# Norm weights as one row spread by products with ones, an early table load, and one PSUM bank for each 32-row merge, in a hybrid DeltaNet / RWKV-7 / Mamba-2 layer

## The chip, the cores and the metric

The program runs on one core of a Trainium2 chip. The metric is the device time of one execution in microseconds. The kernel before takes 1450.17 us (median of three runs, 1448.45 to 1453.15).

Engines: TensorE (PE) multiplies, with its weight loads shown as PEld; VectorE is DVE, ScalarE is ACT, GpSimd is POOL, and SyncE is SP, which here only issues transfers. Each takes its instructions in order. PE writes to PSUM, eight banks of 128 partitions by 512 float32; the other data lie in SBUF.

## The reference

One layer: `h + rms_norm(mixed @ w_out)`, where `h` is 16 meta tokens and 1024 frames of 1024 channels (1040 rows), `hn = rms_norm(h, norm_pre)`, one projection `hn @ w_in` feeds three groups of heads, and `mixed` is what they give, 2048 wide.

```
rms_norm(x, w) = x * rsqrt(mean(x*x) + 1e-6) * w
DeltaNet (6 heads of 128), in chunks:
  A   = strict_lower((k*beta) k^T * decay)
  sol = (A + I)^-1 [v*beta, k*beta*exp(gc)]
  then a scan over the chunks with a 128x128 state
RWKV-7  (8 heads of 64):  S <- S diag(w) + (S a) b^T + v k^T
Mamba-2 (12 heads of 64): chunked scan
```

The two places that matter here are the norm at the start, with its weight `norm_pre` (1024 numbers), and the inverse `(A + I)^-1` of each DeltaNet chunk.

## The kernel before

`setup` loads the rows in nine tiles `x` (c = 0 the 16 meta tokens, c = 1 to 8 each 128 frames), and the weight `npre` as 128 equal rows, which is one transfer that reads the same 4 KB 128 times. `pack` holds small constants in 578 columns, the identity (`ident`) in the first 128. For each tile, ACT squares and sums (L249, the table of activation functions loads ahead of the first), DVE makes the inverse root in a chain of eleven small instructions for each group of tiles `XG` (L252 and the helper), multiplies the tile by it and by `npre` (L256), PE transposes it in two halves of four 128x128 blocks (L261, tile `xT`), ACT copies each half rounded to `hh` (L264), and DVE writes what was lost in the rounding to `hl` (L265). `xT` has two banks, so that the transposes of a tile wait until `hl` of the tile before is written. `b_low` then projects the first 128 columns (`pj`, 72 matmuls), and `scalars` the small ones (`pjs`).

After that a planner written in Python (`schedule`) interleaves units: six DeltaNet heads a0 to a5, four RWKV pairs b0 to b3, two Mamba halves c0 and c1, and at the end the output projection `po`. A unit first projects its columns (each product as three of rounded operands, `hh` and `hl` against two parts of a weight), then it runs its scan on one of two lanes, and projections of later units fill PE between its steps. The planner settles which unit's piece comes next. Each instruction's place on its engine is then settled by a scheduler at compile time, by priorities and its own estimate of what is ready when.

PSUM: four banks `proj` for projections, and two banks for each of the two lanes (`gen0`, `gen1`), handed out in turn by `self.ps`.

The inverse in a DeltaNet head works on two chunks of 64 side by side in 128 rows. A substitution on DVE inverts the 32x32 blocks. Two merges join them to 64: tile `am1` holds 16 products of 32x32 (eight column blocks for each half of the rows), ACT copies them, and `am2` holds 16 products, and eight more for the transposed part. Then `am4` and `am5` join the 64 to 128. Each half has its own bank before, `pair[0]` and `pair[1]`. All matmuls here are issued by one helper, so that the profile gives them line 97; the profile counts two PE instructions for one float32 product. RWKV pairs have the same two merges, `bm1` and `bm2`, with both halves in one bank.

Of the kernel before, what the change touches and what calls it, by code (L numbers as in the profile page):

```python
# [14 lines left out]
F32 = mybir.dt.float32  # L15
F32R = mybir.dt.float32r
I32 = mybir.dt.int32
AF = mybir.ActivationFunctionType
ALU = mybir.AluOpType
MUL, ADD, SUB, MAX = ALU.mult, ALU.add, ALU.subtract, ALU.max  # L20

D = 1024
# [49 lines left out]
def t0(c):  # L72
    return 0 if c == 0 else NM + 128 * (c - 1)


def nt(c):
    return NM if c == 0 else 128
# [24 lines left out]
class Trunk:  # L102
# [102 lines left out]
    def setup(self):  # L205
        nc, a, cp = self.nc, self.a, self.cp
        v, act = nc.vector, nc.scalar
        self.hh = self.hp.tile([128, KT, L], F32R, tag="hh", name="hh")
        self.hl = self.hp.tile([128, KT, L], F32R, tag="hl", name="hl")
        xt = []  # L210

        def load(c):
            t = self.one([128, D], f"x{c}")
            nc.sync.dma_start(t[: nt(c)], a["meta"] if c == 0 else a["x"][128 * (c - 1): 128 * c])
            xt.append(t)

        for c in range(4):
            load(c)
        npre = self.one([128, D], "npre")
        nc.sync.dma_start(npre, a["npre"].broadcast_to((128, D)))  # L220
        pk = cp.tile([128, sum(n for _, n in PACK)], F32, tag="pack", name="pack")
        nc.sync.dma_start(pk, a["pack"])
        o = 0
        for key, n in PACK:
            setattr(self, key, pk[:, o: o + n])
            o += n
        for key, n in (("ctap_a", 18), ("ctap_c", 14)):
            setattr(self, key, getattr(self, key).rearrange("p (i t) -> p i t", i=n))
        for c in range(4, 9):
            load(c)  # L230
        wraw = self.one([128, KT, 32], "ws_raw")
        nc.sync.dma_start(wraw, a["ws"])
        self.ws = w = self.one([128, KT, 64], "ws_hl", F32R)
        nc.gpsimd.tensor_copy(w[:, :, 0:32], wraw)
        nc.gpsimd.tensor_tensor(w[:, :, 32:64], wraw, w[:, :, 0:32].bitcast(F32), SUB)
        self.pk2 = self.one([128, sum(n for _, n in PACK2)], "pack2")
        nc.sync.dma_start(self.pk2, a["pack2"])
        for key, n in (("dtb", 24), ("alog", 18), ("mbd", 12)):
            t = cp.tile([128, n], F32, tag="c_" + key, name="c_" + key)
            nc.sync.dma_start(t, a[key].broadcast_to((128, n)))  # L240
            setattr(self, key, t)
        ss = cp.tile([128, 9], F32, tag="xss", name="xss")
        rs = cp.tile([128, 9], F32, tag="xrs", name="xrs")
        v.memset(ss, 1.0)
        for cc in XG:
            for c in cc:
                n = nt(c)
                junk = self.one([128, D], "xjunk")
                act.activation(junk[:n], xt[c][:n], AF.Square, accum_out=ss[:n, c: c + 1])  # L249
            sl = slice(cc[0], cc[-1] + 1)  # L250
            with self.tc.high_priority(XP):
                v.tensor_scalar(ss[:, sl], ss[:, sl], 1.0 / D, EPS, MUL, ADD)  # L252
                self.rsqrt(rs[:, sl], ss[:, sl], "xr")
            for c in cc:
                n = nt(c)
                v.scalar_tensor_tensor(xt[c][:n], xt[c][:n], rs[:n, c: c + 1], npre[:n], MUL, MUL)  # L256
                for g in range(2):
                    p = self.ps(f"xT{c}_{g}")
                    for k in range(4):
                        kt = 4 * g + k  # L260
                        nc.tensor.transpose(p[:, k * 128: k * 128 + n], xt[c][:n, kt * 128: (kt + 1) * 128], self.ident[:n, :n])  # L261
                    pv = p.rearrange("p (k t) -> p k t", k=4)[:, :, :n]
                    sl = (slice(None), slice(4 * g, 4 * g + 4), slice(t0(c), t0(c) + n))
                    act.copy(self.hh[sl], pv)  # L264
                    v.tensor_tensor(self.hl[sl], pv, self.hh[sl].bitcast(F32), SUB)  # L265

        o = sum(n for _, n in PACK[:-HALVED])
        nc.gpsimd.tensor_scalar(pk[:, o:], pk[:, o:], 0.5, None, MUL)
        self.mu1 = cp.tile([128, 17], F32, tag="mu1", name="mu1")
        nc.gpsimd.tensor_scalar(self.mu1, self.mu, -1.0, 1.0, MUL, ADD)  # L270
        self.ka1 = cp.tile([128, 4], F32, tag="ka1", name="ka1")
        nc.gpsimd.tensor_scalar(self.ka1, self.ka, -1.0, 1.0, MUL, ADD)
# [96 lines left out]
    def unit_a(self, h):  # L369
        nc, sm = self.nc, self.sm  # L370
        v, act, pe, pool, sync = self.engines
# [17 lines left out]
        lo3 = lo[:, NM:].rearrange("p (c t) -> p c t", c=8)  # L389
# [11 lines left out]
        rs = sm.tile([128, 17], F32, tag="a_rs", name="a_rs", bufs=3)  # L401
        v.memset(ss[:, 0:1], 1.0)
        kdec = self.one([128, 8, 128], f"akd{h}")
        for cc, p in transposed(k, "akT", groups):
            for j, c in enumerate(cc):
                n = nt(c)
# [18 lines left out]
        for gi, cc in enumerate(groups):  # L425
            pk = self.ps(f"agk{h}_{gi}")
            for j, c in enumerate(cc):
                n, s = nt(c), t0(c)
                pe.matmul(pk[:n, j * 128: j * 128 + n], k[:, s: s + n], k[:, s: s + n], start=True, stop=True)
            for j, c in enumerate(cc):  # L430
                n, s = nt(c), t0(c)
# [32 lines left out]
        for cc, p in transposed(v_, "avT", groups):  # L464
            for j, c in enumerate(cc):
                n = nt(c)
# [11 lines left out]
        for gi, cc in enumerate(groups[:2]):  # L478
            gq = self.ps(f"agq{h}_{gi}")
            for j, c in enumerate(cc):  # L480
                s = t0(c)
# [7 lines left out]
        dd, v2 = dv[:, 0], dv[:, 1]  # L489
# [6 lines left out]
        v1 = dvf[:, 512:768], dvf[:, 0:256]  # L496
        fs = [(slice(64 * i, 64 * i + 32), slice(64 * i + 32, 64 * i + 64)) for i in range(2)]

        pair = [self.ps(f"am1{h}_{i}") for i in range(2)]
        for c in range(8):  # L500
            for i, (f, s) in enumerate(fs):
                pe.matmul(pair[i][s, 32 * c: 32 * c + 32], lo3[f, c, s], dd[f, c, 0:32], start=True, stop=True)
        for i, (f, s) in enumerate(fs):
            act.copy(v1[i][s], pair[i][s, 0:256])
        yield 0.6
        pair = [self.ps(f"am2{h}_{i}") for i in range(2)]
        for c in range(8):
            for i, (f, s) in enumerate(fs):
                pe.matmul(pair[i][f, 32 * c: 32 * c + 32], v1[i][s, 32 * c: 32 * c + 32], lo3[s, c, s], start=True, stop=True)
        f, s = fs[0]  # L510
        for c in range(8):
            pe.matmul(pair[0][s, 32 * c: 32 * c + 32], lo3[s, c, s], v1[0][s, 32 * c: 32 * c + 32], start=True, stop=True)
        act.copy(dd[s, :, 0:32], pair[0][s, 0:256].rearrange("p (c t) -> p c t", c=8))
        for i, (f, s) in enumerate(fs):
            act.copy(lo3[f, :, s], pair[i][f, 0:256].rearrange("p (c t) -> p c t", c=8))
        yield

        f, s = slice(0, 64), slice(64, 128)
        p = self.ps(f"am4{h}")
# [4 lines left out]
        p = self.ps(f"am5{h}")  # L524
# [16 lines left out]
        for c in range(9):  # L541
            n, s = nt(c), t0(c)
            if c:
                pk = self.ps(f"aks{h}_{c}")
# [44 lines left out]
        for gi in range(2):  # L589
            p = self.ps(f"aoT{h}_{gi}")  # L590
# [808 lines left out]
```

## Time and profile before

| | |
|---|---|
| median of three runs | 1450.17 us |
| the profiled execution | 1442.35 us, its span 1440.4 us |
| PE busy | 1389.7 us, 96% of the span |
| DVE busy | 935.4 us, 65% |
| ACT busy | 719.9 us, 50% |
| granted TensorE clock, mean | 0.985 of full speed |

The profile is one execution: the span goes from the first instruction to the last, and 1.95 us lie around it. Busy time is the time in which an engine has at least one instruction under way; overlapping matmuls count once. A line of the timeline merges equal instructions that follow each other (xN). In a window the clock is the mean of what was granted there. The windows show 1.00 up to 45 us, but transposes take twice as long in the first 25 us as later, so that there the figure is not the clock that the engine had.

### The profile page before, as it was taken

Reading aid. Unit: us, or ns where it says so; the run is one execution under the profiler, and the core shown is the slowest. Engines: PE = TensorE matmul, PEld = TensorE weight load, DVE = VectorE, ACT = ScalarE, POOL = GpSimd, SP = SyncE. Lnnn points to the kernel's source line nnn. Section 1 sums busy time; section 2 is a strip of 40 time slices with the busy share of each in tenths; the row PEclk is TensorE's granted clock in tenths of the full one; section 3 lists DMA queues with packets and bytes.
Section 4 is the critical chain, followed back from the end, with each engine's and each line's share of the span. In section 5 each row is a group of like instructions: output and inputs, shape, how many; then the busy total and the mean of one; then the engine's idle time right before and its main releaser. Section 6 shows DMA issues by size and latency. Waiting matters only on the chain.

```text
span 1440.4 us, 28351 instructions
## 1 busy us (share of the span) xinstructions
PE 1389.7 (96%) x10801; PEld 1188.8 (83%) x10801; DVE 935.4 (65%) x2610; ACT 719.9 (50%) x2020; POOL 172.4 (12%) x223
## 2 busy tenths in 40 slices
PE   4999999999999999999999999999999999899997
PEld 4999888778788789979778898889998987677786
DVE  6548586467667348879625788655589876632663
ACT  6365445446364464545636655444666355632520
POOL 2111010000010011111001110001231110201000
PEclk9999999999999999999979999999999999999999
DMA  7354243213234143234422242234553322743861
GB/s 233 78 131 87 56 102 71 57 40 88 44 66 112 30 133 89 57 82 89 100 60 60 54 108 62 59 88 89 133 124 77 71 38 56 233 133 101 254 198 44
DMA packets 120458, 136.43 MB, mean 95 GB/s; under 512 B 39867, under 2 KB 72379, under 8 KB 120323
## 3 DMA queue, kind: packets, MB, share of 16 engines
q1 hardware_dynamic: 102755, 102.64, 24.1%
q0 software_dynamic: 17568, 31.99, 13.4%
q8 instruction: 85, 1.39, 0.4%
q14 instruction: 50, 0.41, 0.1%
HBM read 116.99 MB, written 17.60 MB: 93 GB/s over the span
## 4 chain that ended last, share of the span: by engine, by line
PE 78%; issue 6%; ACT 6%; DMA 4%; DVE 4%; POOL 0%; SPq 0%; DVEq 0%; ACTq 0%; POOLq 0%
PE pj L97 45%; PE po L97 5%; PE bsi L97 4%; PE bu L97 3%; PE bgr L97 3%; PE am L97 2%; PE aops L97 1%; PE cdg L97 1%; ACT bbt L97 1%; DMA or<-in_w_out_dram 1%; PE ads L97 1%; PE av L97 1%; DMA omrw<-d_mix 1%; PE aks L97 1%; PE agk L97 1%
## 5 line engine op out<-in xcount | busy, mean ns | idle before, releaser
L97 PE MATMUL pj<-hh,w 128*128 128x350 f32 (+7 forms) x2736 | 757.6, 348 | 0.2 <-ACT hh L264 0.2
L97 PEld LDWEIGHTS pj<-hh,w 128*128 128x128 f32 x2736 | 483.4, 190 | 25.7 <-issue 4.4
L97 PE MATMUL pj<-hl,w 128*128 128x350 f32 (+7 forms) x1368 | 474.8, 347 | 0.0
L97 PEld LDWEIGHTS pj<-hl,w 128*128 128x128 f32 x1368 | 260.2, 190 | 11.8 <-issue 1.2
L153 POOL DMA_DIRECT2D w<-in_wt_dram x122 | 106.5, 873 | 878.6 <-ACT w L151 600.5
L151 ACT ACTIVATE w<-wr 128x512 fp32r<-128x512 f32 x122 | 76.8, 630 | 72.7 <-PE pj L97 70.7
L97 PE MATMUL po<-ow,omw 128*128 128x512 f32 x408 | 97.7, 400 | 4.0 <-ACT omw L1088 3.2
L97 PEld LDWEIGHTS po<-ow,omw 128*128 128x128 f32 x408 | 77.5, 191 | 24.2 <-ACT omw L1088 3.6
L97 PE MATMUL po<-ow,ome 128*128 128x512 f32 x360 | 90.5, 402 | 2.1 <-ACT ome L1088 1.6
L97 PEld LDWEIGHTS po<-ow,ome 128*128 128x128 f32 x360 | 66.6, 189 | 17.7 <-ACT ome L1088 2.2
L152 ACT CAST w<-wr 128x512 fp32r<-128x512 f32 x122 | 74.4, 609 | 0.1
L97 DVE TENSOR_SCALAR buv<-bu,b_ib 128x64 f32<-128x64 f32 x68 | 19.2, 282 | 71.6 <-PE bu L97 71.5
L97 PE MATMUL bsi<-buv,bgm 64*64 64x64 f32 x784 | 63.0, 230 | 0.7 <-DVE b_s L97 0.2
L97 DVE TENSOR_TENSOR s_tmp<-alb 33x30 f32<-33x30 f32 (+9 forms) x180 | 57.0, 317 | 3.2 <-DMA alb<-d_l 1.9
L97 DVE TENSOR_TENSOR alb<-alb,s_tmp 33x30 f32<-33x30 f32 (+9 forms) x180 | 57.0, 317 | 3.0 <-POOL alb L97 1.6
L97 PEld LDWEIGHTS bsi<-buv,bgm 64*64 64x64 f32 x784 | 43.5, 136 | 16.5 <-issue 4.6
L184 DVE SCALAR_TENSOR_TENSOR cbc<-pj,pack,cbc 128x346 f32<-128x346 f32 (+4 forms) x72 | 41.1, 571 | 20.5 <-ACT cbc L181 19.7
L852 ACT COPY by<-bsi 64x64 f32<-64x64 f32 x128 | 26.5, 207 | 48.9 <-PE bsi L97 47.6
L1089 DVE TENSOR_TENSOR ome<-omre,ome 128x512 fp32r<-128x512 f32 (+2 forms) x40 | 22.5, 600 | 36.2 <-ACT ome L1088 36.1
L97 PE MATMUL bgr<-bar,bbk 64*64 64x128 f32 x544 | 45.4, 277 | 0.0
L97 PE MATMUL bu<-buv,bbt 64*64 64x64 f32 x512 | 42.4, 234 | 0.0
L184 DVE SCALAR_TENSOR_TENSOR cx<-pj,pack,cx 128x346 f32<-128x346 f32 (+2 forms) x54 | 31.1, 576 | 16.9 <-ACT cx L181 15.9
(324 smaller groups left out, 2390.3 us busy)
## 6 DMA issues: line engine op xcount, KB each, us to landing
wr<-in_wt_dram SPq DMA_DIRECT2D x122, 256.0 KB, 3.4
w<-in_wt_dram POOLq DMA_DIRECT2D x122, 256.0 KB, 4.8
or<-in_w_out_dram SPq DMA_DIRECT2D x32, 256.0 KB, 3.8
omrw<-d_mix SPq DMA_DIRECT2D x32, 256.0 KB, 3.9
clt<-d_cs SPq DMA_DIRECT2D x24, 256.0 KB, 4.9
omre<-d_mix SPq DMA_DIRECT2D x24, 256.0 KB, 2.8
btw<-d_tw SPq DMA_DIRECT2D x8, 544.0 KB, 5.9
x<-in_x_dram SPq DMA_DIRECT2D x8, 512.0 KB, 7.7
```

The costliest lines, as they stand in the source:

```text
L97: return op(out, *args, **kw)
L151: nc.scalar.activation(w[:, 1], raw, AF.Copy, scale=-1.0)
L152: nc.scalar.copy(w[:, 0], raw)
L153: nc.gpsimd.dma_start(w[:, 1], src, accum_op=ADD)
L184: nc.vector.scalar_tensor_tensor(acc[:, a + z: b], p[:, o + z - s: o + b - a - s], cw[:, 3 - s: 4 - s], acc[:, a + z: b], MUL, ADD)
L852: nc.scalar.copy(yt[hs[(c - 1) % 2], (c - 1) // 2, hs[h]], pq[hs[h], 64:128])
L1089: nc.vector.tensor_tensor(t[:, 1], raw, t[:, 0].bitcast(F32), SUB)
```

## The change

The weight comes as one row of 1024 numbers by ACT's queue. Beside it in the same tile stand 128 ones, written by POOL and squared by ACT. Two products with one row in the contraction, ones against the row, put `npre` on 128 partitions of two `proj` banks, and L256 becomes two instructions of 512 columns that read the weight from PSUM. The square of the ones is the first activation in the program, so the table loads ahead of it. The identity comes by ACT's queue, the rest of `pack` by SP's. In the merges, both halves of `am1` share a bank, and both halves of `am2`.

```diff
--- before.py
+++ after.py
@@ -214,19 +214,28 @@
             nc.sync.dma_start(t[: nt(c)], a["meta"] if c == 0 else a["x"][128 * (c - 1): 128 * c])
             xt.append(t)
 
+
+        row = self.one([1, D + 128], "npre")
+        nc.scalar.dma_start(row[:, 0:D], a["npre"])
+        nc.gpsimd.memset(row[:, D:], 1.0)
+        act.activation(row[:, D:], row[:, D:], AF.Square)
         for c in range(4):
             load(c)
-        npre = self.one([128, D], "npre")
-        nc.sync.dma_start(npre, a["npre"].broadcast_to((128, D)))
         pk = cp.tile([128, sum(n for _, n in PACK)], F32, tag="pack", name="pack")
-        nc.sync.dma_start(pk, a["pack"])
+        nc.scalar.dma_start(pk[:, 0:128], a["pack"][:, 0:128])
+
+        npre = [self.pp.tile([128, 512], F32, tag="proj", name=f"npre{g}") for g in range(2)]
+        for g in range(2):
+            nc.tensor.matmul(npre[g], row[:, D:], row[:, 512 * g: 512 * g + 512], start=True, stop=True)
         o = 0
         for key, n in PACK:
             setattr(self, key, pk[:, o: o + n])
             o += n
         for key, n in (("ctap_a", 18), ("ctap_c", 14)):
             setattr(self, key, getattr(self, key).rearrange("p (i t) -> p i t", i=n))
-        for c in range(4, 9):
+        load(4)
+        nc.sync.dma_start(pk[:, 128:], a["pack"][:, 128:])
+        for c in range(5, 9):
             load(c)
         wraw = self.one([128, KT, 32], "ws_raw")
         nc.sync.dma_start(wraw, a["ws"])
@@ -253,8 +262,9 @@
                 self.rsqrt(rs[:, sl], ss[:, sl], "xr")
             for c in cc:
                 n = nt(c)
-                v.scalar_tensor_tensor(xt[c][:n], xt[c][:n], rs[:n, c: c + 1], npre[:n], MUL, MUL)
                 for g in range(2):
+                    xg = xt[c][:n, 512 * g: 512 * g + 512]
+                    v.scalar_tensor_tensor(xg, xg, rs[:n, c: c + 1], npre[g][:n], MUL, MUL)
                     p = self.ps(f"xT{c}_{g}")
                     for k in range(4):
                         kt = 4 * g + k
@@ -496,23 +506,23 @@
         v1 = dvf[:, 512:768], dvf[:, 0:256]
         fs = [(slice(64 * i, 64 * i + 32), slice(64 * i + 32, 64 * i + 64)) for i in range(2)]
 
-        pair = [self.ps(f"am1{h}_{i}") for i in range(2)]
+        p = self.ps(f"am1{h}")
+        for c in range(8):
+            for f, s in fs:
+                pe.matmul(p[s, 32 * c: 32 * c + 32], lo3[f, c, s], dd[f, c, 0:32], start=True, stop=True)
+        for i, (f, s) in enumerate(fs):
+            act.copy(v1[i][s], p[s, 0:256])
+        yield 0.6
+        p = self.ps(f"am2{h}")
         for c in range(8):
             for i, (f, s) in enumerate(fs):
-                pe.matmul(pair[i][s, 32 * c: 32 * c + 32], lo3[f, c, s], dd[f, c, 0:32], start=True, stop=True)
-        for i, (f, s) in enumerate(fs):
-            act.copy(v1[i][s], pair[i][s, 0:256])
-        yield 0.6
-        pair = [self.ps(f"am2{h}_{i}") for i in range(2)]
-        for c in range(8):
-            for i, (f, s) in enumerate(fs):
-                pe.matmul(pair[i][f, 32 * c: 32 * c + 32], v1[i][s, 32 * c: 32 * c + 32], lo3[s, c, s], start=True, stop=True)
+                pe.matmul(p[f, 32 * c: 32 * c + 32], v1[i][s, 32 * c: 32 * c + 32], lo3[s, c, s], start=True, stop=True)
         f, s = fs[0]
         for c in range(8):
-            pe.matmul(pair[0][s, 32 * c: 32 * c + 32], lo3[s, c, s], v1[0][s, 32 * c: 32 * c + 32], start=True, stop=True)
-        act.copy(dd[s, :, 0:32], pair[0][s, 0:256].rearrange("p (c t) -> p c t", c=8))
-        for i, (f, s) in enumerate(fs):
-            act.copy(lo3[f, :, s], pair[i][f, 0:256].rearrange("p (c t) -> p c t", c=8))
+            pe.matmul(p[s, 32 * c: 32 * c + 32], lo3[s, c, s], v1[0][s, 32 * c: 32 * c + 32], start=True, stop=True)
+        act.copy(dd[s, :, 0:32], p[s, 0:256].rearrange("p (c t) -> p c t", c=8))
+        for f, s in fs:
+            act.copy(lo3[f, :, s], p[f, 0:256].rearrange("p (c t) -> p c t", c=8))
         yield
 
         f, s = slice(0, 64), slice(64, 128)
```

Where the instructions stand. The SP queue at its start (`x` tiles in the order meta, 1, 2, ...; tile numbers differ between the kernels), before:

```order
L214 DMA x_81<-in_meta_dram 16x1024
L214 DMA x_83<-in_x_dram 128x1024
L214 DMA x_85<-in_x_dram 128x1024
L214 DMA x_87<-in_x_dram 128x1024
L220 DMA npre<-in_npre_dram 128x1024
L222 DMA pack<-in_pack_dram 128x578
L214 DMA x_93<-in_x_dram 128x1024
L214 DMA x_95<-in_x_dram 128x1024
```

and now:

```order
L237 DMA pack<-in_pack_dram 128x450
L214 DMA x_85<-in_meta_dram 16x1024
L214 DMA x_87<-in_x_dram 128x1024
L214 DMA x_89<-in_x_dram 128x1024
L214 DMA x_91<-in_x_dram 128x1024
L214 DMA x_99<-in_x_dram 128x1024
L214 DMA x_102<-in_x_dram 128x1024
L214 DMA x_104<-in_x_dram 128x1024
```

The second part of `pack` stands ahead of the meta tokens, although the code has it after tile 4; nothing stands between the tiles any more.

ACT at its start, before (`xT_0` and `xT_1` are the two halves of a tile's transposes; `xss` collects the sums of squares):

```order
L249 ACT_TABLE_LOAD
L249 ACTIVATE xjunk,xss<-x_81 16x1024
L249 ACTIVATE xjunk,xss<-x_83 128x1024
L249 ACTIVATE xjunk,xss<-x_85 128x1024
L249 ACTIVATE xjunk,xss<-x_87 128x1024
L249 ACTIVATE xjunk,xss<-x_93 128x1024
L249 ACTIVATE xjunk,xss<-x_95 128x1024
L264 CAST hh<-xT_0_136 128x4x16
L264 CAST hh<-xT_1_143 128x4x16
L249 ACTIVATE xjunk,xss<-x_97 128x1024
```

and now:

```order
L219 DMA npre<-in_npre_dram 1x1024
L221 ACT_TABLE_LOAD
L221 ACTIVATE npre<-npre 1x128
L225 DMA pack<-in_pack_dram 128x128
L258 ACTIVATE xjunk,xss<-x_85 16x1024
L258 ACTIVATE xjunk,xss<-x_87 128x1024
L258 ACTIVATE xjunk,xss<-x_89 128x1024
L258 ACTIVATE xjunk,xss<-x_91 128x1024
L258 ACTIVATE xjunk,xss<-x_99 128x1024
L274 CAST hh<-xT_0_143 128x4x16
L258 ACTIVATE xjunk,xss<-x_102 128x1024
L274 CAST hh<-xT_1_151 128x4x16
```

The first rounded copy `hh` of the meta tokens stands behind five squares, where it stood behind six, and the second half behind one more.

PE in the fifth head's merges, before (`am_0_12730` and `am_1_12731` are the two banks of `am1`, `am_0_12774` and `am_1_12775` those of `am2`; `pj` fills, `avT` are transposes; one more group of eight of `am1` stands 19 rows further up):

```order
L97 MATMUL pj_0_13233<-hh,w_0_13112 128x512
L97 MATMUL am_1_12731<-add_12723,alo_11791 32x32 x8
L97 MATMUL pj_0_13233<-hl,w_0_13112 128x512
L97 MATMUL pj_0_13233<-hh,w_0_13112 128x512 x2
L97 MATMUL am_0_12774<-alo_11791,add_12723 32x32 x8
L97 MATMUL am_0_12774<-add_12723,alo_11791 32x32 x8
L97 MATMUL avT_0_13245<-pack,av_12670 128x128 x2
L97 MATMUL avT_1_13259<-pack,av_12670 128x128
L97 MATMUL pj_0_13233<-hl,w_0_13112 128x512
L97 MATMUL pj_0_13233<-hh,w_0_13112 128x512
L97 MATMUL am_1_12775<-alo_11791,add_12723 32x32 x8
L97 MATMUL pj_0_13233<-hh,w_0_13112 128x512
```

and now (`am_12738` is `am1`, `am_12781` is `am2`, and one product of `am1` stands 19 rows further up):

```order
L97 MATMUL pj_0_13239<-hh,w_0_13118 128x512
L97 MATMUL am_12738<-add_12731,alo_11799 32x32 x15
L97 MATMUL pj_0_13239<-hl,w_0_13118 128x512
L97 MATMUL pj_0_13239<-hh,w_0_13118 128x512 x2
L97 MATMUL avT_0_13251<-pack,av_12678 128x128 x2
L97 MATMUL avT_1_13265<-pack,av_12678 128x128
L97 MATMUL pj_0_13239<-hl,w_0_13118 128x512
L97 MATMUL am_12781<-alo_11799,add_12731 32x32 x16
L97 MATMUL am_12781<-add_12731,alo_11799 32x32 x8
L97 MATMUL pj_0_13239<-hh,w_0_13118 128x512
```

Eight products of one half after eight of the other have become runs of 15 and 16 in which, as the code's loop has it, the halves take turns. Over the six heads the 32x32 products stand in 25 runs before, and in 23 now. Apart from the two products of the weight, all other instructions of PE are the same; from the first head's merges on many have swapped places with their neighbours.

## Rows read from the trace of the kernel before

**Rows 1.** The page, span and busy us (share, instructions).

```profile
span 1440.4 us, 28351 instructions
...
PE 1389.7 (96%) x10801; PEld 1188.8 (83%) x10801; DVE 935.4 (65%) x2610; ACT 719.9 (50%) x2020; POOL 172.4 (12%) x223
```

**Rows 2.** Busy us by stretch (instructions), then clock, DMA share.

```profile
0.00:45.00 45.00, 26.30 (x152) 23.79 (x153) 28.57 (x79) 28.07 (x54) 8.84 (x17) 1.00 0.62 189
...
45.00:150.00 105.00, 104.48 (x723) 98.37 (x720) 70.20 (x194) 52.81 (x141) 15.32 (x23) 0.98 0.45 101
...
1200.00:1300.00 100.00, 92.02 (x526) 71.55 (x525) 50.22 (x124) 49.15 (x132) 13.14 (x10) 0.98 0.43 135
```

**Rows 3.** Waits of PE: total us, times, longest.

```profile
PE xT L261 <- DVE x L256: 11.1, 1, 11.1
...
PE xT L261 <- DVE hl L265: 7.4, 5, 2.7
```

**Rows 4.** Timeline of the start: start, us, engine, operation [idle before <-releaser].

```profile
2.94 1.28 ACT L249 ACT_TABLE_LOAD   x1 [2.94 <-DMA x<-in_meta_dram]
...
8.18 1.06 ACT L249 ACTIVATE xjunk<-x 128x1024 f32<-128x1024 f32 x1 [0.72 <-DMA x<-in_x_dram]
...
8.42 0.16 DVE L97 SCALAR_TENSOR_TENSOR xrs<-xr_t,xrs 128x2 f32<-128x2 f32 x1
...
9.73 1.27 DVE L256 SCALAR_TENSOR_TENSOR x<-x,xrs,npre 16x1024 f32<-16x1024 f32 x1 [1.15 <-DMA npre<-in_npre_dram]
...
10.93 0.15 DVE L252 TENSOR_SCALAR xss<-xss 128x2 f32<-128x2 f32 x1
...
11.92 1.06 ACT L249 ACTIVATE xjunk<-x 128x1024 f32<-128x1024 f32 x1 [2.60 <-DMA x<-in_x_dram]
...
14.48 0.23 DVE L265 TENSOR_TENSOR hl<-xT,hh 128x64 fp32r<-128x64 f32 x1 [2.01 <-ACT hh L264]
...
14.76 1.97 PE L261 MATMUL xT<-pack,x 128*128 128x128 f32 x8 [2.67 <-DVE hl L265]
...
31.19 1.03 PE L261 MATMUL xT<-pack,x 128*128 128x128 f32 x8
...
43.59 0.31 PE L97 MATMUL pj<-hh,w 128*128 128x322 f32 x1
```

**Rows 5.** Groups by form: count, busy us, mean ns, idle before.

```profile
L256 DVE SCALAR_TENSOR_TENSOR x<-x,xrs,npre 128x1024 f32<-128x1024 f32 x8 | 10.2, 1277 | 0.0
...
L97 DVE SCALAR_TENSOR_TENSOR az<-aoT,pack,az 128x512 f32<-128x512 f32 x12 | 8.6, 744 | 0.9 <-PE aoT L97 0.9
...
L97 PE MATMUL bbon<-bat,pack 128*128 128x512 f32 x16 | 8.5, 612 | 0.3 <-ACT buv L97 0.3
```

**Rows 6.** Timeline, first merge of a DeltaNet head, two banks.

```profile
168.19 0.69 PE L97 MATMUL am<-add,alo 32*32 32x32 f32 x16
...
168.81 0.44 PE L97 MATMUL pj<-hh,w 128*128 128x386 f32 x1
...
169.18 0.69 PE L97 MATMUL am<-add,alo 32*32 32x32 f32 x16
```

**Rows 7.** Timeline, merge of an RWKV pair, halves alternating, one bank.

```profile
231.51 0.75 PE L97 MATMUL bm<-bdd,bgm 32*32 32x32 f32 x34
...
232.19 0.44 PE L97 MATMUL pj<-hh,w 128*128 128x386 f32 x1
```

**Rows 8.** Timeline, second merge of the fifth head, halves one after the other.

```profile
1147.73 0.69 PE L97 MATMUL am<-alo,add 32*32 32x32 f32 x16
...
1148.34 0.50 PE L97 MATMUL pj<-hh,w 128*128 128x512 f32 x1
```

**Rows 9.** Busy us by stretch, a part at the lower clock.

```profile
721.00:724.00 3.00, 3.00 (x78) 2.78 (x78) 0.00 (x0) 1.49 (x6) 0.00 (x0) 0.95 0.43 175
...
727.00:730.00 3.00, 3.00 (x20) 1.95 (x20) 0.28 (x1) 1.08 (x3) 0.00 (x0) 0.50 0.00 0
...
739.00:742.00 3.00, 3.00 (x25) 2.48 (x25) 1.07 (x4) 1.06 (x5) 0.00 (x0) 0.70 0.00 0
```


## The prediction

> **What bounds the kernel now.** I read the page first, for the share of each engine, then the busy times by stretch, for where the engine that sets the time stands idle, then what PE waited for, and last the timeline of those places. PE is busy for 1389.7 of 1440.4 us [rows 1], so 50.7 us are to be had without less work for PE. In the first 45 us it is busy for 26.30: 18.7 us of idle time, more than a third of the whole, lie there [rows 2]. From 45 to 150 us it is busy for 104.48 of 105, since projections of later units fill every gap; time won before 44 us is therefore not lost again soon, and less work for PE shortens that part one for one. From 1200 to 1300 it is busy for 92.02 of 100: there the chains between engines decide.
>
> In the setup PE waits 11.1 us for the first tile that DVE has multiplied, and 7.4 us in five waits for `hl` [rows 3]. The timeline shows why. The inverse root of the first group ends at 8.42 + 0.16 = 8.58, but DVE starts its first multiplication at 9.73, when `npre` has landed. ACT stands for 2.60 us until tile 4 lands at 11.92, squares it and tile 5, and only then makes the first `hh`; DVE waits 2.01 us for that [rows 4]. Behind 14.5 us DVE has work nearly all the time, and PE follows it. The last product of `b_low` starts at 43.59. So the setup is bound by loads first, then by DVE.
>
> **The change, part by part: the setup.** Gone are `npre`'s 512 KB, and `pack` (289 KB) has left the place between tiles 3 and 4. Between the landing of `npre` and that of tile 4 lie 2.19 us for 801 KB (pack and tile 4), 366 KB in a us [rows 4]. Tile 4 would now come 512/366 = 1.4 us behind tile 3, at 9.6. But the order shows the second part of `pack` (450 columns, 225 KB) ahead of all tiles: 0.6 us later for each. I take 9.8, since the wide transfer of `npre`, which also slowed what ran beside it, is gone.
>
> The first multiplication needs the root of tiles 0 and 1, and these come up to 0.6 us later; the root ends at 8.6 to 9.2 instead of being ready at 8.58 and waiting till 9.73. Gain 0.5 to 1.1, I take 0.8. The table load (1.28 us, from 2.94) moves ahead of the first tile's landing, but I cost that at nothing: tile 1's square, not the meta tokens', ends the group, and it waits for its load. If tile 1 had been there early, up to 1.28 us would be won.
>
> The first `hh` now stands behind the square of tile 4 instead of tile 5. With tile 4 at 9.8 and about 1.05 us for a square it comes at 10.9 instead of 14.2, and of the wait of 2.01 us some 0.6 stay. Gain 1.4.
>
> Against this stand the halves. A multiplication of 1024 columns holds DVE for 10.93 - 9.73 = 1.20 us to the next start, though it lasts 1.277. A half that reads one operand from PSUM has its like in the rows of `az<-aoT`, 744 ns [rows 5]; with the same overlap of 0.07 that is 0.67, and 1.34 for two. Nine tiles: 9 x 0.14 = 1.2 us lost, and DVE is the bound there. Sum of the setup: 0.8 + 1.4 - 1.2 = 1.0 us gained. Its ends: if all loads come 1.5 us late and the halves cost all they can, a loss of 0.7; if `pack` costs nothing and the halves overlap like whole ones, a gain of 2.5.
>
> Cost at nothing: the two products that spread the row. A float32 product of 512 columns is two PE instructions of 612 ns [rows 5], and eight transposes last 1.97 us at 14.76 but 1.03 at 31.19 [rows 4], so that PE runs at half speed early: 2 x 2 x 0.61 x 2 = 4.9 us at most. The row stands first in ACT's queue and should land with the meta tokens, at about 3; the weight is there at 8, before the root. Behind these products only transposes wait, which need DVE anyway. If the row lands 2 us later, about 1 us of the gain goes. The two banks of `proj` that hold the weight come free with tile 8's multiplication, before the third piece of `b_low` wants one. The square of the ones waits for POOL's memset, with the squares of the tiles behind it, which have not landed then.
>
> **The merges.** Sixteen PE instructions of one half, one after the other, hold PE from 168.19 to 168.81, 39 ns each [rows 6]. Thirty-four that take turns between halves in one bank hold it from 231.51 to 232.19, 20 ns each [rows 7]. `am1` has 32: before 2 x 0.62 = 1.24 us a head; now 2 at 39 and 30 at 20, 0.68. Six heads: 3.4 us. In `am2` the halves took turns before already in the first four heads; in the last two they stand one after the other (0.61 us for one half, [rows 8]) and go from 1.24 to 0.64, 1.2 us in two. Each run also costs the projection beside it: 0.37 us from 168.81 to 169.18 for 386 columns, which stream in 386/2400 = 0.16, an estimate from the full clock. With 25 runs before and 23 now that is another 0.4. The sum, 5.0, holds where PE is full. The sixth head lies in the stretch from 1200 us where PE is not; its 1.2 I leave out, and 0.3 for places at which a swapped neighbour waits: 3.5 us. The ends are 0 and 5.0.
>
> The Trainium skill, TensorEngine Tiling (Array Packing), Gotcha 1: PSUM Pressure, speaks against this part: different row tiles cannot access the same PSUM bank simultaneously. By that rule the two halves, whose inputs lie in different rows, would go one after the other in a shared bank, and the 3.5 us would be 0. This case's trace does not agree: the RWKV merges run at 20 ns each in one shared bank [rows 7].
>
> Together 1.0 + 3.5 = 4.5 us. The profiled execution would go from 1442.35 (span 1440.4 and 1.95 around it) to 1437.9. The median of the runs stands 7.8 us above that execution; from it, 1450.17 - 4.5 = 1445.7.
>
> **The rivals.**
>
> First, the merges bring nothing, because the halves do not overlap in one bank or because the swapped neighbours wait as long as was won. For it: PE's order has changed in many places behind the first merge, and nothing in the trace prices that. Against it: rows 7, and PE's full stretches. Time: 1450.17 - 1.0 = 1449.2.
>
> Second, the clock. From 724 to 739 us the granted clock is 0.50 in every stretch of 3 us, five of them, with 0.95 before (0.3 us at the lower level) and 0.70 behind (1.8 us) [rows 9]: 17.1 us at 1.2 instead of 2.4 GHz, in which PE lost about half, 8.5 us. Just ahead of the fall stand 78 PE instructions in 3 us, small products of the second head's merges for the most part. If shorter runs spare this stretch, the time is 1445.7 - 8.5 = 1437.2. Against it: other runs of the same kind pass without a fall.
>
> Third, slower: the same mechanism the other way. The swapped order behind the second head's merges (718 us) puts its small products beside those of a neighbouring RWKV pair, and one more stretch of 17.1 us falls to the lower clock. Time: 1445.7 + 8.5 = 1454.2. It decides from 2 x 4.5 = 9 us more at the lower clock, where the whole gain is gone. For it: the runs of the kernel before differ by 4.7 us among themselves, so something of this size comes and goes. Against it: the small products become fewer microseconds, not more.
>
> Fourth, the setup does not gain: `pack` in front and the halves eat what the loads give, -0.7. Time: 1450.17 + 0.7 - 3.5 = 1447.4.
>
> **How the numbers follow.** Chances: forecast 0.47 (its own range 1443 to 1448.5), merges bring nothing 0.14, lower clock spared 0.15, one more stretch of it 0.16, setup without gain 0.08. A change over 0.3%, 4.35 us, is what a measurement of this kernel can tell: below 1445.8 is faster, above 1454.5 slower. Faster: 0.27 of the forecast, 0.15, and 0.02 of the fourth, 0.44. Slower: 0.11 of the third, where any part of the saving is missing. Within: the other 0.45. The range takes in the second and third rivals' times with the bounds of the unknown costs, 1437 to 1454; 0.17 stays outside.
>
> **What would show it.** In the changed profile DVE's first multiplication starts near 8.8, tile 4's square near 9.8, and the first `hh` near 10.9; a half multiplication lasts about 744 ns; the last product of `b_low` starts near 42.6. Wrong if that is 43.6 or later. The runs of `am1` hold PE for about 20 ns an instruction; at 39 the merge part is wrong. A lower clock at 724 to 739, or another stretch like it, tells the second and third rivals. If all these come as forecast and the time is still above 1449, the swapped order behind the merges is what I have not priced.

## The result, and the profile after

The changed kernel takes 1435.82 us (median of 20 runs, 1430.25 to 1450.65), the kernel before 1446.74 in 20 runs beside it. The ratio is 0.9929 with a 95% interval of 0.9912 to 0.9945: 10.3 us less (8 to 13), where 4.5 were forecast, and below the range's lower end of 1437.

Of the changed kernel the page gives, as in [rows 1], the span and the busy us:

```profile
span 1442.0 us, 28374 instructions
...
PE 1393.5 (97%) x10805; PEld 1188.9 (82%) x10805; DVE 935.9 (65%) x2619; ACT 719.8 (50%) x2021; POOL 170.3 (12%) x224
```

This execution is 1.6 us longer than the one profiled of the kernel before, and PE is busy for 3.8 us more. It took 1443.86 us, 8 above the median, and its mean clock is 0.980, where the 20 runs lie between 0.978 and 0.991 and most near 0.988. So one profile against one profile does not give the gain. Time by stretch, as in [rows 2] (busy PE, PEld, DVE, ACT, POOL, then clock and DMA):

```profile
0.00:45.00 45.00, 32.20 (x164) 25.77 (x165) 29.63 (x88) 29.98 (x56) 8.28 (x19) 1.00 0.61 183
45.00:150.00 105.00, 104.50 (x722) 98.58 (x721) 71.37 (x197) 51.55 (x140) 14.44 (x22) 0.98 0.44 99
...
450.00:600.00 150.00, 147.41 (x1341) 125.28 (x1340) 87.57 (x212) 71.07 (x203) 19.32 (x24) 0.95 0.34 83
...
1200.00:1300.00 100.00, 91.24 (x518) 70.65 (x517) 51.19 (x127) 48.16 (x130) 12.80 (x10) 0.97 0.44 138
1300.00:1450.00 150.00, 128.28 (x531) 102.09 (x530) 70.17 (x183) 41.69 (x86) 8.12 (x6) 0.94 0.45 142
```

In the first 45 us PE is busy for 32.20 instead of 26.30, of which 3.8 are the two products of the weight. The 0.95 from 450 and the 0.94 at the end, where the kernel before's profile has 0.99 and 0.97, are what makes this execution long.

The places of [rows 4] and [rows 5] in the changed kernel's start (timeline, then groups by form):

```profile
3.02 3.77 PE L229 MATMUL npre<-npre 1*128 1x512 f32 x4 [3.02 <-ACT npre L221]
...
8.14 1.06 ACT L258 ACTIVATE xjunk<-x 128x1024 f32<-128x1024 f32 x1 [0.93 <-DMA x<-in_x_dram]
...
9.47 0.73 DVE L267 SCALAR_TENSOR_TENSOR x<-x,xrs,npre 16x512 f32<-16x512 f32 x1
...
10.70 1.06 ACT L258 ACTIVATE xjunk<-x 128x1024 f32<-128x1024 f32 x1
...
11.76 0.19 ACT L274 CAST hh<-xT 128x64 fp32r<-128x64 f32 x1
...
11.98 0.23 DVE L275 TENSOR_TENSOR hl<-xT,hh 128x64 fp32r<-128x64 f32 x1 [0.50 <-ACT hh L274]
...
42.38 0.31 PE L97 MATMUL pj<-hh,w 128*128 128x322 f32 x1
```

```profile
L267 DVE SCALAR_TENSOR_TENSOR x<-x,xrs,npre 128x512 f32<-128x512 f32 x16 | 11.7, 740 | 0.0
```

The weight is there at 6.8. The squares of tiles 2 and 4 start at 8.14 and 10.70, the first multiplication at 9.47, the first `hh` at 11.76, and DVE waits 0.50 us for it instead of 2.01; the last product of `b_low` starts at 42.38 instead of 43.59.

The fifth head's merges, as in [rows 8] (timeline of PE):

```profile
1141.66 0.69 PE L97 MATMUL am<-add,alo 32*32 32x32 f32 x30
1142.28 0.50 PE L97 MATMUL pj<-hl,w 128*128 128x512 f32 x1
```

Thirty instructions of `am1` in 0.62 us, 21 ns each, against 39 in [rows 6]. And the place of [rows 9], from 724 us on:

```profile
724.00:730.00 6.00, 6.00 (x111) 4.12 (x109) 0.28 (x1) 2.76 (x7) 0.00 (x0) 1.00 0.45 179
730.00:736.00 6.00, 6.00 (x61) 4.49 (x62) 0.86 (x3) 3.32 (x10) 0.86 (x1) 1.00 0.32 65
736.00:742.00 6.00, 6.00 (x56) 4.83 (x55) 1.96 (x6) 2.27 (x10) 0.00 (x0) 1.00 0.14 26
```

The second head's merges lie here too, and the clock stays at 2.4 GHz: the 17.1 us at 1.2 GHz are gone.

### The profile page after: what moved, and what is told of

It reads as the page before. It is cut to its first block, busy times and chain, and to the rows that moved or that the text cites. A ratio compares the mean times of both kernels' runs of the same rounds, so it can differ in the third digit from the quotient of the medians.

```text
span 1442.0 us, 28374 instructions
## 1 busy us (share of the span) xinstructions
PE 1393.5 (97%) x10805; PEld 1188.9 (82%) x10805; DVE 935.9 (65%) x2619; ACT 719.8 (50%) x2021; POOL 170.3 (12%) x224
## 4 chain that ended last, share of the span: by engine, by line
PE 85%; ACT 5%; DMA 4%; DVE 4%; issue 1%; POOL 0%; SPq 0%; DVEq 0%; ACTq 0%; POOLq 0%
PE pj L97 47%; PE po L97 10%; PE bsi L97 4%; PE bu L97 3%; PE bgr L97 3%; PE am L97 2%; PE aops L97 1%; PE cdg L97 1%; ACT bbt L97 1%; DMA omrw<-d_mix 1%; PE ads L97 1%; PE av L97 1%; PE agk L97 1%; DMA or<-in_w_out_dram 1%; PE aks L97 1%
```

## Experiments

Each run of a kernel gives a time and a mean clock. Beside the runs of the study stand 104 of the kernel before with a clock: 1447.4 us in the median, mean clock 0.981. A straight line through all 269 runs (one slope, an offset for each kernel) gives 1.11 us for 0.001 of mean clock, with a scatter of 1.7 us. This splits a gain in two: what comes with the clock, and what is left at equal clock, called work below. Its error is 0.4 to 0.8 us, and the split may be rougher than that: in the runs below the work of two parts of the merges comes to 5.3 and to 4.6 us, where all merges together have 3.0.

**The kernel before again, and the two halves of the change.**

> The kernel before, unchanged, so that the granted clock of each of its runs is seen. In the two profiled runs the change is worth 3.9 us beside the clock (at the last output product the start moves by +1.2 us, while the stretches at 1.2 GHz up to there cost 25.6 - 20.5 = 5.1 us more). Theory 'work and clock': the rest of the 10.3 us between the medians is time at the lower clock, so this kernel's runs show a lower mean clock than the changed kernel's 0.988: about 0.983, and time plus 1419 us x (clock - 1) some 4 us above the changed kernel's 1418. Theory 'all work': the mean clock is 0.988 as in the changed kernel, and that sum lies 10 us higher. Ratio 1.000 under both.

> The setup's change alone, merges as before. Theory 'work and clock, from the merges': 1.2 us less (the first products of the small weights started at 42.4 instead of 43.6 us), ratio 0.9992, clock as the kernel before. Rival 'setup carries it' (the earlier start also shifts which stretches fall to the lower clock): most of the 10 us, ratio 0.994 or less, clock near 0.988.

> The merges' change alone, setup as before. Theory 'work and clock, from the merges': 2.7 us of work and some 6 us of spared lower clock, ratio 0.9937, mean clock near 0.988. Rival 'setup carries it': 2.7 us of work or less, ratio 0.998, clock as the kernel before.

> The whole change again, beside its parts on the same chip. If the parts add up: ratio 0.993, clock near 0.988, and its gain is the sum of the two parts' gains within 2 us. If the parts help each other (a shifted phase of the clock), the whole gains over 3 us more than the sum.

The edit is the diff's hunks for `setup` alone, or that for the merges alone. Measured: the kernel before 1.0009 (0.9985 to 1.0032), clock 0.980; setup alone 0.9970 (0.9952 to 0.9989), clock 0.985, between its two expectations and so run again below; merges alone 0.9941 (0.9915 to 0.9966), clock 0.986; the whole change 0.9919 (0.9887 to 0.9951), clock 0.987. At equal clock the setup is worth 0.8 us, the merges 3.0, the whole 5.6 here and 4.8 in the first 20 runs. The gains of the parts, 4.3 and 8.5 us by the ratios, make up the 11.7 of the whole within 2. So the gain is work and clock, and most of it comes with the merges; the theory that all is work is out. One mean of 40 us around the second head's merges tells where the clock differs. Kernel before, setup alone, merges alone:

```profile
712.00:752.00 40.00, 39.86 (x443) 30.17 (x444) 11.31 (x41) 17.03 (x53) 1.75 (x2) 0.79 0.23 68
```

```profile
712.00:752.00 40.00, 39.86 (x423) 30.31 (x418) 11.19 (x40) 16.74 (x53) 1.74 (x2) 0.79 0.25 70
```

```profile
712.00:752.00 40.00, 39.86 (x501) 31.18 (x501) 15.70 (x59) 21.72 (x69) 2.98 (x4) 1.00 0.32 91
```

PE is idle for 0.14 of the 40 us in each; 0.79 is 17 of them at the lower level.

**Which step, and is it the bank?**

```diff
 e4: am1 as after, am2 as before        e5: am1 as before, am2 as after
 e6: both in one bank, but
-        for c in range(8):
-            for f, s in fs:
+        for f, s in fs:
+            for c in range(8):
```

> Setup as before; only the first merge step (am1) shares a bank, am2 keeps two. In the profile of the changed kernel am1 holds PE for 2.6 us less over six heads and am2 for 2.0 us less (4.65 us together). Theory 'am1's halves at 39 ns bring the fall': the 17.1 us at 1.2 GHz near 724 are gone, work 2 us less, ratio 0.995 and mean clock near 0.986. Rival 'am2 brings it': the stretch stays, ratio 0.9985, clock near 0.981.

> The counterpart: only am2 shares a bank, am1 keeps two. Theory 'am1 brings the fall': the 17.1 us at 1.2 GHz near 724 stay, work 1.2 us less, ratio 0.999, mean clock 0.981. Rival 'am2 brings it': the stretch is gone, ratio 0.995, clock near 0.986. If both parts alone remove it, the sum of the time in small products decides, not one step.

> Setup as before; the merges share a bank, but one half's eight products stand ahead of the other's in the code, so that no two halves take turns. Theory 'taking turns is what saves' (20 ns against 39 ns an instruction): the 4.65 us of PE time come back, the stretch near 724 is there again, ratio 1.000, clock 0.981. Rival 'the bank is what saves' (one bank fewer to wait for): the instructions hold PE as long as before, but the stretch is gone and the ratio is 0.996 or less.

Measured: `am1` alone 0.9933 (0.9907 to 0.9959), clock 0.985; `am2` alone 0.9946 (0.9918 to 0.9974), clock 0.984; halves one after the other 0.9985 (0.9952 to 1.0017), clock 0.980. The same 40 us of the three:

```profile
712.00:752.00 40.00, 39.86 (x528) 30.36 (x526) 16.77 (x64) 23.18 (x84) 2.61 (x3) 1.00 0.33 93
```

```profile
712.00:752.00 40.00, 39.86 (x469) 30.24 (x469) 12.52 (x45) 18.32 (x57) 1.75 (x2) 0.83 0.19 60
```

```profile
712.00:752.00 40.00, 39.86 (x438) 30.59 (x437) 12.31 (x51) 17.85 (x58) 0.86 (x1) 0.74 0.23 67
```

With `am1` changed the fall is gone; with `am2` changed it stays; with one bank and no turns it stays too. In this last kernel sixteen instructions of one half hold PE as in [rows 6]:

```profile
878.37 0.69 PE L97 MATMUL am<-add,alo 32*32 32x32 f32 x16
878.99 0.42 PE L97 MATMUL pj<-hh,w 128*128 128x350 f32 x1
```

So it is the turns that save, 39 ns against 21; sharing a bank only brings them about. The kernel before bears this out: its second head's `am2` has two banks, the halves take turns in most of a run of 29 instructions, and these take 0.69 us, 24 ns each (the rows from 721.81 to 722.50 below). At equal clock `am1` alone is worth 3.2 us where 2 were expected, `am2` alone 2.1 where 1.2 were, and one bank without turns 0.8; with an error of 0.5 each, only the first is more than two errors off. The ratio of `am2` alone is lower than expected (0.999), since its mean clock is above the kernel before's though its one profile has the fall; this part is not explained.

**The second head alone, and all others.**

```diff
+        if h == 1:      # the other kernel: if h != 1
+            p = self.ps(f"am1{h}")
...
+        else:
             pair = [self.ps(f"am1{h}_{i}") for i in range(2)]
```

> The kernel before, with the new merges in the second head alone (the one whose products stand ahead of the 17.1 us at 1.2 GHz near 724). Its PE time saved is 2.75 - 2.25 = 0.5 us. Theory 'that stretch is the missing part of the gain': it is gone, mean clock up by 17.1/2/1440 = 0.006 to about 0.986, 0.5 + 6.6 us less, ratio 0.995. Rival 'work in all heads': ratio 0.9995, clock 0.980.

> The counterpart: the new merges in all heads but the second. Theory 'that stretch is the missing part': it stays near 722, clock 0.980 to 0.981, and only the work of five heads is won, 4.65 - 0.5 = 4.1 us of PE time of which 2.5 to 3 count: ratio 0.998. Rival 'work in all heads': ratio 0.9945 as with all six.

Measured: the second head alone 0.9951 (0.9917 to 0.9984), clock 0.986; the other five 0.9996 (0.9977 to 1.0015), clock 0.979. The same 40 us of the two:

```profile
712.00:752.00 40.00, 39.86 (x516) 30.64 (x515) 16.71 (x64) 23.04 (x82) 2.60 (x3) 1.00 0.33 94
```

```profile
712.00:752.00 40.00, 39.87 (x449) 29.63 (x447) 14.02 (x56) 18.87 (x66) 1.72 (x2) 0.79 0.24 67
```

One head's merges, 0.5 us of PE time, bring 7 us (2 to 12), at equal clock 1.2. The five others, with eight times as much PE time, bring 0.6 (from 2 us lost to 3 won): 3.4 us of work at equal clock, hidden by a mean clock a little below that of the kernel before. Neither of these is what work in all heads would give (0.9995 for the one, 0.9945 for the five): the missing part of the gain is the stretch near 724.

**The start.**

```diff
 e8 and e12 (the same kernel):
-        nc.sync.dma_start(pk[:, 128:], a["pack"][:, 128:])
         for c in range(5, 9):
             load(c)
+        nc.gpsimd.tensor_copy(pk[0:1, 128:129], xt[3][0:1, 0:1])
+        nc.sync.dma_start(pk[:, 128:], a["pack"][:, 128:])
 e9, on top of it:
+            v.tensor_copy(wide[:, 512 * g: 512 * g + 512], npre[g])
...
-                    ... npre[g][:n], MUL, MUL)
+                    ... wide[:n, 512 * g: 512 * g + 512], MUL, MUL)
```

> The whole change, with the second part of the packed constants (450 columns) behind the tiles of x instead of ahead of them (POOL writes one element of it from tile 3, so its load must wait). Theory 'pack in front delays the tiles': tile 2's square starts 0.6 us or more earlier than at 8.14, the first DVE multiply near 8.9 instead of 9.47, and the last product of b_low 0.5 us earlier; ratio 0.9915. Rival 'the rate of the loads is the same, and DVE sets the end': the first multiply moves, the end of b_low does not; ratio as the changed kernel's.

> As with the constants behind the tiles, and the spread weight is first copied by VectorE from PSUM to SBUF (two copies of 512 columns, at about 5.5 and 6.8), so that the 18 half multiplications read SBUF alone. Theory 'reading PSUM is what makes a half dear': a half falls from 0.74 to about 0.64 us (half of the 1.277 of a whole one), 18 x 0.1 = 1.8 us of DVE, less some 0.5 us that the second copy delays the root; the last product of b_low comes 0.5 to 1 us earlier than 41.5. Rival 'the fixed part of an instruction': a half stays above 0.7 us and b_low's last product comes at 41.5 or later.

> The setup's change alone, once more, for a second profile and more clocks. In its first runs the mean clock was 0.9846 against 0.980 of the kernel before, more than the stretches of its one profile explain (they explain about 1.5 of some 5 us: an earlier rise and no fall near 36 us). If that is an effect of the change: 0.984 to 0.985 again, ratio 0.997. If it was chance: 0.980 to 0.982, ratio 0.998 to 0.999. The 17.1 us at 1.2 GHz near 724 should be there again under both; if they are missing, the setup's change spares them in some executions, and that is the missing part.

> The whole change once more, beside the two versions that go further: ratio 0.9925, mean clock 0.987, no stretch at 1.2 GHz near 720 and b_low's last product at 42.3.

> The constants behind the tiles once more, on the same chip as the whole change: b_low's last product at 41.5, 0.8 us earlier than in the whole change; ratio to the kernel before 0.991 to 0.992, time 0.5 to 1.5 us under the whole change's. If that is not seen, the clock's spread hides it.

Constants behind the tiles: 0.9891 (0.9854 to 0.9927), again 0.9917 (0.9887 to 0.9947); the whole change beside the second of these 0.9912 (0.9882 to 0.9942). In its two profiles tile 2's square starts at 7.56 and 7.93, and `b_low`'s last product at:

```profile
41.47 0.31 PE L97 MATMUL pj<-hh,w 128*128 128x322 f32 x1
```

```profile
42.11 0.31 PE L97 MATMUL pj<-hh,w 128*128 128x322 f32 x1
```

The whole change has it at 42.38, 42.29 and 43.19 in three profiles. So `pack` in front costs up to a microsecond there, which the times cannot tell. The copy to SBUF did not help: 0.9936 (0.9901 to 0.9971), `b_low`'s last product at 44.67, and a half that reads SBUF alone takes as long:

```profile
L271 DVE SCALAR_TENSOR_TENSOR x<-x,xrs,nprew 128x512 f32<-128x512 f32 x16 | 11.8, 743 | 0.0
```

The setup alone, once more: 0.9987 (0.9961 to 1.0012), clock 0.982, with the fall in the same place. The first 0.985 was part chance; over both series the setup has 0.983 and 1.2 us of work (0.8 and 1.5). The whole change has 3.7 here, and 4.8 over its three series.

## Why the prediction was wrong, point by point

**The step that failed is the clock.** The sum has no term for it: it leaves the 17.1 us at 1.2 GHz [rows 9] where they are and puts sparing them into the second rival, at 0.15, with "other runs of the same kind pass without a fall" against it. That rival is what happened: the stretch is gone, and the mean clock went from 0.981 to 0.987. At 1.11 us for 0.001 that is some 7 us beside the 4.8 of work, and the two make up the 11.6 us between the medians, 1447.4 and 1435.8. The fall is not there by chance in one execution: it stands behind or in the second head's merges in all seven profiles of kernels in which this head's `am1` has its halves one after the other, and in none of the nine in which they take turns. What differs in this head is what stands around it. Ahead of the fall PE ran, before (timeline):

```profile
720.94 0.69 PE L97 MATMUL am<-add,alo 32*32 32x32 f32 x16
721.55 0.32 PE L97 MATMUL bsi<-b_s,bar 64*64 64x64 f32 x2
721.81 0.87 PE L97 MATMUL am<-alo,add 32*32 32x32 f32 x29
722.50 0.21 PE L97 MATMUL am<-add,alo 32*32 32x32 f32 x1
...
723.60 0.71 PE L97 MATMUL pj<-hl,w 128*128 128x512 f32 x1
```

From 720.94 on no projection has a product until 723.60, 2.7 us. In the kernel with this head changed alone, a piece of that place reads:

```profile
724.97 0.62 PE L97 MATMUL am<-add,alo 32*32 32x32 f32 x26
725.52 0.33 PE L97 MATMUL bu<-buv,bbt 64*64 64x64 f32 x4
725.69 0.28 PE L97 MATMUL bsi<-buv,bgm 64*64 64x64 f32 x4
725.90 0.73 PE L97 MATMUL pj<-hh,w 128*128 128x512 f32 x2
...
728.65 0.50 PE L97 MATMUL pj<-hl,w 128*128 128x512 f32 x1
```

`am1` is over sooner, with the projection's products close behind it, and the small products that follow last from 726.56 to 728.65, 2.1 us. The run with `am1` ahead of these two products has grown in turn, from 2.0 us to 2.4. So the longest run without a projection that holds these merges is 2.7 to 3.2 us in the seven profiles with the fall, and 2.4 in the nine without. That this length is what brings the fall is not shown. No run changes it alone, and longer runs, of products on 64 rows, pass at 2.4 GHz in the same profile: from 381.75 to 385.68 no projection has a product, and the clock is 1.00.

```profile
381.00:387.00 6.00, 5.91 (x94) 4.71 (x94) 2.81 (x7) 2.37 (x8) 0.86 (x1) 1.00 0.46 87
```

What the runs show is that the order of the second head's `am1` decides; why the clock falls behind one order and not behind the other stays open. The profile did point at the place: [rows 9] showed 78 PE instructions in the 3 us ahead of the fall, and the change was to shorten just those. I counted the other heads as evidence that such runs do no harm, but their 32x32 products stand among projections. The Trainium skill, TensorE: Matmul & The Clock Gate, Part 1, says that the gate follows how busy PE has been. The busy time of the trace does not tell this fall: PE is busy for 3.00 of 3.00 us as the clock falls [rows 9].

**The sum held, at equal clock, but not its terms.** Setup forecast 1.0, measured 1.2; merges 3.5, measured 3.0; together 4.5, measured 4.8, as far as the split into work and clock can tell. An instruction of the merges takes 21 ns, forecast 20. Within the merges two terms were off and made up for each other: over the six heads `am1` holds PE for 2.6 us less, where 3.4 were worked out, since its products stand in several short runs in some heads, and `am2` for 2.0 less, where 1.2 were [rows 6 to 8]. By the Trainium skill, TensorEngine Tiling (Array Packing), Gotcha 1: PSUM Pressure, two halves in different rows could not use one bank at the same time, and this part would have been 0; the trace does not agree, two halves that take turns in one bank go at 21 ns, two that don't at 39 in the same bank. The first rival is out.

**The size of that rival.** 8.5 us took half of the 17.1 as lost. The second head alone brought 7.1, of which 0.0055 of mean clock is 6.1. So the rival, counted from the median of the 104 runs, would have been 1447.4 - 4.5 - 6.1 = 1436.8.

**The base.** 1450.17 is a median of three runs; the 104 others have 1447.4. From there the forecast would have been 1443 and the range's lower end 1434.3.

**The setup's steps.** The sum came out, its account did not. DVE's first multiplication was to start 0.8 us sooner; it starts at 9.40 to 9.75 in the eight profiles with the old setup and at 9.47 to 10.68 in the five with the new one, so nothing was won there, and without this term the sum would have been 0.2. That 1.2 was measured, with an error of 0.4, is in part luck. The weight no longer holds it up, but the first tiles come later: the squares of tiles 1 and 2 start at 6.06 and 8.14 instead of 5.29 and 6.33, where 0.6 us for `pack` in front were counted. With `pack` behind the tiles tile 2's still starts at 7.56 and 7.93, so `pack` is the smaller part of this delay; no run shows what the rest is, and none bears out that the wide transfer of `npre` had slowed what ran beside it. Tile 4's square starts at 10.70 (9.8 forecast) and the first `hh` at 11.76 (10.9), since ACT has three squares in a row. The wait of DVE for this `hh` went as forecast, from 2.01 to 0.50 us (0.6 forecast). `b_low` ends sooner all the same, and by more than the one profile of before shows: its last product starts at 43.59 there [rows 4], but in another execution of the same kernel at

```profile
45.79 0.31 PE L97 MATMUL pj<-hh,w 128*128 128x322 f32 x1
```

and over eight profiles with the old setup at 45.2 in the mean, with five of the new one at 42.7. In that execution the clock fell again soon after it rose, 0.89 in this window where before's profile has 1.00. Five of the eight profiles with the old setup have this fall, and none of the eight with a new one, so that a part of the 2.5 us is clock:

```profile
30.00:45.00 15.00, 13.37 (x81) 12.69 (x79) 8.95 (x13) 6.35 (x13) 0.00 (x0) 0.89 0.11 28
```

The price of a half was right (0.744 forecast, 0.740), but that it reads PSUM is not the reason for it: from SBUF it is the same (0.743).

**The other rivals.** No further stretch of 17.1 us at 1.2 GHz came up at a fixed place, so the third is out. Something of its kind is there at a fifth of the size. A fall near 1220 us lasts twice as long in nine of the ten profiles of kernels whose other heads have both halves of `am1` in one bank, and in none of the six others; before and after:

```profile
1205.00:1235.00 30.00, 27.11 (x215) 20.29 (x214) 17.73 (x52) 17.61 (x48) 5.13 (x4) 0.94 0.30 101
```

```profile
1205.00:1235.00 30.00, 25.89 (x211) 19.47 (x209) 15.91 (x45) 18.39 (x55) 5.09 (x4) 0.89 0.41 137
```

That is some 3 us more at the lower level, and it fits that the other five heads alone have a mean clock a little below the kernel before's. The fourth is out: it has the setup lose 0.7 us, and over its two series the setup gains 1.2 of work with an error of 0.4, though the second ratio by itself would allow it.

**What stays open.** Why the clock falls behind one order of the second head's `am1`. And why `am2` alone and the setup alone have a mean clock 0.003 above the kernel before's while their profiles keep the fall. The profiles explain less than half: with `am2` alone the fall is 13.6 us long instead of 16.8 by the rows of 40 us, and the new setup lacks the fall near 36 us. A profile shows one execution in many, and the short stretches at 1.2 GHz lie elsewhere in each. No version tried is faster than the changed kernel by more than its runs can tell.

## What to carry to other kernels

When PE is full, look at where the granted clock falls in the profile and at what PE ran just ahead of it: a change to those products can be worth the fall and not only its own microseconds (0.5 us of PE time, 7 us of time here, 2 to 12). Check with a second profile whether such a stretch stands behind the same instructions each time before calling it chance. And forecast from the median of many runs, since one profile and three times can both lie some microseconds off.

## What the runs showed of the hardware that was not expected

- The clock fell to 1.2 GHz while the profile had PE without a gap, behind 32x32 and 64x64 products, and came back only 14 to 20 us later. It did so in all seven profiles with one order of 32 of these products, and in none of nine with another.
- Two halves of the rows that take turns in one PSUM bank go at 21 ns a PE instruction; the same products half after half at 39, in one bank or in two. A run in which they take turns in two banks for the most part goes at 24.
- A scalar_tensor_tensor of 512 float32 columns takes 0.74 us whether its weight lies in PSUM or in SBUF, and one of 1024 takes 1.28: two halves last 0.2 us more, and it is not PSUM that makes them dear.
